# Turning the first attention's latent rows with VectorE's block transposes and HBM instead of TensorE

## The chip, the cores and the metric

The kernel runs on one core of one Trainium2 chip. The metric is device time in microseconds (us). Before the change the median of three runs is 802.17 us (801.53 to 802.32).

The engines are PE (TensorE, matmuls; PEld is its weight load), DVE (VectorE), ACT (ScalarE), POOL (GpSimd) and SP (SyncE, whose queue here issues nearly all DMAs). Each engine works through its own queue in order and waits on semaphores that other engines and DMAs set.

## The reference, cut to what matters

Two layers over 256 tokens of width 1024, all in float32. Each layer has a mixer with three branches and an MLP:

```python
for l in range(2):
    h = rms_norm(x, attn_norm[l])
    x = x + hybrid_mixer(h, ...)          # MLA | MoBA | retention, gated, then w_out
    h = rms_norm(x, mlp_norm[l])
    x = x + square(relu(h @ w_up)) @ w_down
return rms_norm(x, final_norm)

# in hybrid_mixer: p = h @ w_in, split; of it the first attention (MLA) takes 256 + 128 + 32 columns
cq, ckv = rms_norm(cq, q_norm_g), rms_norm(ckv, kv_norm_g)       # the latents, 256 and 128 wide
q = cq @ w_q_up                       # 8 heads x (64 plain + 32 for the rope)
kv = ckv @ w_kv_up                    # 8 heads x (64 key + 64 value)
k = concat(kv's key part, rope(k_rope) broadcast to all heads)
o = softmax(causal(q k^T * 96**-0.5)) v
```

`rms_norm(x, g) = x * rsqrt(mean(x^2) + eps) * g`, so a norm's weight `g` can be applied to the rows or, since it belongs to an input column of the next matmul, to the rows of the next weight matrix.

## The kernel before

**Arithmetic.** Every float32 operand of a matmul is split into a high part (rounded to the fast float32 format) and a low part (the rest), and a product is three matmuls, high by high, high by low, low by high (`three`, lines 298 to 300). A weight block arrives by DMA in `raw` (7 buffers of 128x1024), ACT copies its high part `whi` (line 277), DVE subtracts for `wlo` (line 279), both with 6 buffers; this is `fetch`. `load_w` fetches one block ahead. The order of the blocks in HBM is `weight_plan`.

**Order of the work.** A layer is a list `prog` of units. Most units are a quarter of a projection with 512 output columns: two slices of 128 rows of weights, two token tiles, three matmuls each, so 12 matmuls of 512 columns. `slot(name, j)` finds a unit and `at` hangs a step behind it. Program order gives the priorities; a planner at build time puts each engine's instructions in the order in which, by its own cost estimates, their inputs are ready, the earlier in program order first. A few places are pinned (PE's `manual_schedule`, `keep_in_program_order`, `issue_after`). So a unit's place in PE's queue is fixed when the kernel is built, and on the chip PE waits if its operands come later than planned.

**Around the change.** The units run: b0 (the 416 columns of the latents and the rope key; in the first layer within "start", together with mq), mq, mk, then mv with three units of the first attention among its quarters, then the gates gmla0, gmla1, gmoba0, gmoba1, and the rest (retention, its gate, the branches, wout, the MLP). The steps that the change touches:

- `c_copies`, `c_squares`, `c_norms`: the latent rows (token rows on partitions) in `c0`, their norms (POOL's power), the roped key copied into `krx`, and the rows scaled by their norm (DVE, line 824).
- `c_turn`: for the matmuls that follow, the latents must stand with their columns on partitions. PE transposes six 128x128 tiles of `c0` and two of `krx` into two PSUM tiles `pct` (lines 927 and 930); ACT and DVE split them to `cTh`, `cTl`, applying the norms' weights (`split` with `gain`, lines 314 and 315); ACT copies the roped key to all heads in `KK` (lines 934, 935).
- `qrope`, `qnope`, `kvup` are the units that read `cTh` and `cTl`: the query's rope part (PSUM tile `pqr`), its plain part and the keys (`nope`), the values (`pv`). `qrope` stands ahead of mv's first quarter, the others each a quarter later. `qr_rope` ropes the queries.
- `moba_rope`, `written_rows`, `read_turned`, `fetch_turned`: the second attention's queries and keys already go another way. DVE transposes rows within blocks of 32x32 (line 328), SP writes the blocks to HBM (`rowsbounce`, line 492), and four reads (line 500) bring them back so that the blocks stand in their places. `order_queries` (ACT, line 508) then puts them in order.
- `first = slot("mv", 3)`: where the first attention's first four scores stand; its other steps are counted from there.
- The end of the last layer (lines 1548 to 1568): for each of two token tiles the squares of the two halves (ACT), their multiplication by the final norm's weights (DVE), root, reciprocal, scaling (DVE 640 columns, ACT 384), and two stores.

Of the kernel before, what the change touches and what calls it, by code (L numbers as in the profile page):

```python
# [7 lines left out]
F32 = mybir.dt.float32  # L8
# [3 lines left out]
ALU = mybir.AluOpType  # L12
# [14 lines left out]
LEAD = 10  # L27

SEVEN = [(0, 1, 2, 3, 4, 6)] * L
EPS = 1e-6  # L30
GN_EPS = 1e-5
NEG_INF = -1e30
# [38 lines left out]
def weight_plan():  # L71
# [3 lines left out]
    def block(key, name, kt, cols, per):  # L75
        for j in range(0, kt, per):
            plan.append(((*key, j // per), name, (j, per), cols))
# [4 lines left out]
    for l in range(L):  # L82
# [12 lines left out]
        for i, (key, name, kt, cols) in enumerate(  # L95
            (("qrope", "mla_w_q_up", 2, C_QROPE), ("qnope", "mla_w_q_up", 2, C_QNOPE), ("kvup", "mla_w_kv_up", 1, C_KV))
        ):
            block((l, key), name, kt, cols, kt)
            plan.append(mv[i])
        plan.append(mv[3])  # L100
        for i in range(2):
            block((l, "gmla%d" % i), "w_in", KD, span(C_GMLA + 512 * i, 512), 2)
# [47 lines left out]
def trunk(ctx: ExitStack, tc: tile.TileContext, gx, wts, consts, gfin, gn, xtok, out):  # L150
# [112 lines left out]
    def fetch(key):  # L263
        if key[1] == "down" and key[2] // 4 in SEVEN[key[0]] and key[2] % 4 > 1:
            return fetch_sums(key)
        offset, n, c = where[key]
        sz = n * c
        raw = started.pop(key, None)
        if raw is None:
            raw = wp.tile([P, 1024], F32, name="raw", bufs=RAW)  # L270
            transfer(key, raw)
        hi = wp.tile([P, 1024], F32R, name="whi", bufs=6)
        lo = wp.tile([P, 1024], F32R, name="wlo", bufs=6)
        edge = {"b0mq": 416, "mq": 256}.get(key[1], sz) if key[0] == 0 else sz
        parts = (slice(0, edge), slice(edge, sz)) if edge < sz else (slice(0, sz),)
        for cs in parts:
            fetched.append(nc.scalar.activation(hi[:, cs], raw[:, cs], AF.Copy))  # L277
        for cs in parts:
            nc.vector.tensor_sub(lo[:, cs], raw[:, cs], hi[:, cs].bitcast(F32))  # L279
        return (  # L280
            hi[:, :sz].rearrange("p (k c) -> p k c", k=n),
            lo[:, :sz].rearrange("p (k c) -> p k c", k=n),
        )
# [18 lines left out]
    def gain(c):  # L302
        return G[:, c : c + 1]
# [481 lines left out]
    def layer(l, xn, before):  # L785
# [21 lines left out]
        def c_norms():  # L807
# [4 lines left out]
            for t, (ct, m) in enumerate(c0):  # L812
# [9 lines left out]
                    nc.vector.tensor_copy(dst[:, :, 16 * i : 16 * i + 16], kr[:, 0, :, :])  # L822
                for i, cs in enumerate((slice(0, MLA_QR), slice(MLA_QR, MLA_QR + MLA_KVR))):
                    nc.vector.tensor_scalar(ct[:, cs], ct[:, cs], m[:, 4 + i : 5 + i], s, op0=ALU.mult, op1=ALU.mult)

        if l:
            project(l, "b0", xn, 416, b0.extend, before, ((0,), (1,)))
# [87 lines left out]

        def c_turn():
            c["h"], c["l"] = t4("cTh"), t4("cTl")
            mla["Q"] = sb.tile([P, MLA_H, S], F32, name="Q", bufs=1)  # L920
            KK = mla["K"] = sb.tile([P, MLA_H, S], F32, name="KK", bufs=1)
            mla["v"] = [w2k("vml") for _ in range(NT)]
            pts = [misc_tile("pct") for _ in range(2)]
            for k in range(3):
                pt = pts[k // 2][:, (k % 2) * S : (k % 2) * S + S]
                for t in range(NT):
                    nc.tensor.transpose(pt[:, P * t : P * t + P], c0[t][0][:, P * k : P * k + P], ident)
            pkr = pts[1][:, S : 2 * S]
            for t in range(NT):
                nc.tensor.transpose(pkr[:, P * t : P * t + P], krx[t], ident)  # L930
            for k in range(3):
                pt = pts[k // 2][:, (k % 2) * S : (k % 2) * S + S]
                split(pt, c["h"][:, k, :], c["l"][:, k, :], gain(G_CQ + 3 * l + k))
            nc.scalar.copy(KK[0:64, 1::2, :], pkr[0:64, None, :].to_broadcast([64, 4, S]))
            nc.scalar.copy(KK[64:P, 0::2, :], pkr[64:P, None, :].to_broadcast([64, 4, S]))

        at(slot("mk", 1 if l else 2), c_turn)

        def nope(dst, w, ks, copy, bank):
            for b in range(2):  # L940
# [46 lines left out]

        project(l, "mv", xn, 512, moba_done("mv"))
        for i, unit in enumerate((qrope, qnope, kvup)):
            prog.insert(slot("mv", i), ((unit.__name__, 0), unit))  # L990
        at(slot("mv", 0), qr_rope)

        omlaT, omobaT, oretT = [], [], []
        th_mla = gates(l, "gmla", xn)
        for i, key in enumerate(("mq", "mk")):
            at(slot("mv", i), lambda key=key: moba_rope(key))
            at(slot("gmla0", 2 * i), lambda key=key: fetch_turned(key))
        first = slot("mv", 3)
        at(first, lambda: omlaT.extend((t4("omlah"), t4("omlal"))))

        def mla_scores(h0):
# [27 lines left out]
            qkT["q", h0] = in_order(qkT["mq"], h0 // 2)  # L1029

        for i in range(2):
            at(slot("gmla1", 1 + i), lambda i=i: order_queries(4 * i))
        first = slot("gmoba1", 1)
        at(first, lambda: omobaT.extend((t4("omobah"), t4("omobal"))))

# [511 lines left out]
        for t in range(NT):  # L1547
# [3 lines left out]
            for half in range(2):  # L1551
# [5 lines left out]
                square(acc, 3 * t + half)  # L1557
                if half == 0:
                    nc.vector.tensor_scalar(s2, s0, EPS, None, op0=ALU.add)
                nc.vector.tensor_mul(y[:, cs], acc, gf[:, cs])  # L1560
            nc.scalar.activation(s1, s1, AF.Sqrt, bias=s2)
            nc.vector.reciprocal(r, s1)
            cs = slice(0, 640)
            nc.vector.tensor_scalar(y[:, cs], y[:, cs], r, None, op0=ALU.mult)
            nc.sync.dma_start(out[:, t, cs], y[:, cs])
            cs = slice(640, D)
            nc.scalar.activation(y[:, cs], y[:, cs], AF.Copy, scale=r)
            nc.scalar.dma_start(out[:, t, cs], y[:, cs])
        order_pe.close()
# [116 lines left out]
```

## Time and profile before

| | |
|---|---|
| runs | 802.17 us median of 3, 801.53 to 802.32 |
| the profiled execution's own time | 802.15 us |
| its span (first to last instruction) | 800.0 us |
| mean granted TensorE clock | 0.999 of full speed |
| DVE busy | 655.9 us (82%) |
| ACT busy | 493.7 us (62%) |
| POOL busy | 29.0 us (4%) |
| DMA moved | 194.74 MB, mean 243 GB/s |

A profile is one execution. A row of a timeline reads: start in us from the span's start, duration in us, engine, line, operation, tiles written and read, sizes, count; in brackets how long the engine had been idle and what released it. Several instructions that follow each other can be merged in one row with a count. Matmuls are pipelined: one starts while the one before is in flight, so the distance between starts is what a matmul takes of PE's time, not its duration.

### The profile page before, as it was taken

Reading aid. Unit: us, or ns where it says so; the run is one execution under the profiler, and the core shown is the slowest. Engines: PE = TensorE matmul, PEld = TensorE weight load, DVE = VectorE, ACT = ScalarE, POOL = GpSimd, SP = SyncE. Lnnn points to the kernel's source line nnn. Section 1 sums busy time; section 2 is a strip of 40 time slices with the busy share of each in tenths; the row PEclk is TensorE's granted clock in tenths of the full one; section 3 lists DMA queues with packets and bytes.
Section 4 is the critical chain, followed back from the end, with each engine's and each line's share of the span. In section 5 each row is a group of like instructions: output and inputs, shape, how many; then the busy total and the mean of one; then the engine's idle time right before and its main releaser. Section 6 shows DMA issues by size and latency. Waiting matters only on the chain.

```text
span 800.0 us, 11134 instructions
## 1 busy us (share of the span) xinstructions
PE 793.3 (99%) x3818; PEld 660.3 (83%) x3818; DVE 655.9 (82%) x1131; ACT 493.7 (62%) x750; POOL 29.0 (4%) x32
## 2 busy tenths in 40 slices
PE   9999999999999999999999999999999999999997
PEld 7888887888888888888898888888888888888885
DVE  6779678878888888887796976788698879899795
ACT  7786665454557666666487865654545666666562
POOL 0100000000030000000020000000000300000000
PEclk9999999999999999999999999999999999999999
DMA  9979958965677767787746989598665687788751
GB/s 337 367 234 306 312 206 222 313 217 171 227 220 235 265 235 239 259 270 231 245 148 213 282 292 293 175 274 263 216 221 195 197 273 268 226 274 311 263 189 53
DMA packets 70280, 194.74 MB, mean 243 GB/s; under 512 B 8016, under 2 KB 28112, under 8 KB 70224
## 3 DMA queue, kind: packets, MB, share of 16 engines
q1 hardware_dynamic: 69648, 193.30, 73.2%
q10 hardware_dynamic: 576, 0.74, 0.2%
q8 instruction: 30, 0.49, 0.2%
q14 instruction: 26, 0.21, 0.1%
HBM read 171.46 MB, written 22.02 MB: 242 GB/s over the span
## 4 chain that ended last, share of the span: by engine, by line
PE 99%; ACT 0%; DVE 0%; issue 0%
PE acc L298 19%; PE acc L300 19%; PE acc L299 19%; PE pup L300 8%; PE pup L299 8%; PE pup L298 8%; PE acc L1240 6%; PE acc L859 2%; PE ps_s L1005 1%; PE po L645 1%; PE ps_s L551 1%; PE warm L765 0%; PE po L647 0%; PE b L865 0%; PE ps_r L551 0%; PE b L866 0%
## 5 line engine op out<-in xcount | busy, mean ns | idle before, releaser
L277 ACT ACTIVATE whi<-raw 128x1024 fp32r<-128x1024 f32 (+3 forms) x263 | 265.2, 1020 | 169.6 <-PE acc L300 105.9
L279 DVE TENSOR_TENSOR wlo<-raw,whi 128x1024 fp32r<-128x1024 f32 (+3 forms) x263 | 305.2, 1176 | 72.2 <-ACT whi L277 70.0
L298 PE MATMUL acc<-whi,xs 128*128 128x512 f32 (+1 forms) x384 | 150.0, 392 | 0.0
L299 PE MATMUL acc<-wlo,xs 128*128 128x512 f32 (+1 forms) x384 | 149.4, 389 | 0.0
L300 PE MATMUL acc<-whi,xs 128*128 128x512 f32 (+1 forms) x384 | 149.0, 389 | 0.0
L299 PE MATMUL pup<-wlo,xs 128*128 128x512 f32 x256 | 99.8, 390 | 0.0
L300 PE MATMUL pup<-whi,xs 128*128 128x512 f32 x256 | 99.6, 389 | 0.0
L298 PE MATMUL pup<-whi,xs 128*128 128x512 f32 x256 | 99.4, 389 | 0.0
L298 PEld LDWEIGHTS acc<-whi,xs 128*128 128x128 f32 x384 | 72.1, 188 | 15.7 <-ACT whi L277 0.7
L300 PEld LDWEIGHTS acc<-whi,xs 128*128 128x128 f32 x384 | 72.1, 188 | 14.3
L299 PEld LDWEIGHTS acc<-wlo,xs 128*128 128x128 f32 x384 | 72.1, 188 | 14.0
L300 PE MATMUL acc<-whi,sq 128*128 128x512 f32 x184 | 71.9, 391 | 0.0
L298 PE MATMUL acc<-whi,sq 128*128 128x512 f32 x184 | 71.8, 390 | 0.0
L299 PE MATMUL acc<-wlo,sq 128*128 128x512 f32 x184 | 71.6, 389 | 0.0
L300 PEld LDWEIGHTS pup<-whi,xs 128*128 128x128 f32 x256 | 48.0, 188 | 9.8
L299 PEld LDWEIGHTS pup<-wlo,xs 128*128 128x128 f32 x256 | 48.1, 188 | 9.8
L298 PEld LDWEIGHTS pup<-whi,xs 128*128 128x128 f32 x256 | 48.0, 188 | 9.8
L300 PEld LDWEIGHTS acc<-whi,sq 128*128 128x128 f32 x184 | 34.6, 188 | 7.7 <-DVE sq L319 0.6
L299 PEld LDWEIGHTS acc<-wlo,sq 128*128 128x128 f32 x184 | 34.6, 188 | 7.2
L298 PEld LDWEIGHTS acc<-whi,sq 128*128 128x128 f32 x184 | 34.5, 188 | 7.0
L573 ACT ACTIVATE prob<-prob,smx 128x128 f32<-128x128 f32 x64 | 28.3, 444 | 18.6 <-DVE smx L570 18.5
L1240 PE MATMUL acc<-mT,whi 128*128 128x512 f32 (+1 forms) x144 | 35.2, 371 | 0.0
(277 smaller groups left out, 1206.4 us busy)
## 6 DMA issues: line engine op xcount, KB each, us to landing
raw<-wts SPq DMA_DIRECT2D x264, 512.0 KB, 4.9
bounce<-hblocks SPq DMA_DIRECT2D x16, 512.0 KB, 3.8
hturned<-bounce SPq DMA_DIRECT2D x64, 128.0 KB, 3.0
pbounce<-blocks SPq DMA_DIRECT2D x8, 768.0 KB, 5.8
probT<-pbounce SPq DMA_DIRECT2D x32, 192.0 KB, 5.3
raw<-wts SPq DMA_DIRECT2D x5, 464.0 KB, 6.0
raw<-wts SPq DMA_DIRECT2D x4, 416.0 KB, 4.2
dec<-consts SPq DMA_DIRECT2D x2, 768.0 KB, 7.6
```

What stands on the lines that cost most here:

```text
L277: fetched.append(nc.scalar.activation(hi[:, cs], raw[:, cs], AF.Copy))
L279: nc.vector.tensor_sub(lo[:, cs], raw[:, cs], hi[:, cs].bitcast(F32))
L298: nc.tensor.matmul(o, ah, bh, start=start, stop=False, **more)
L299: nc.tensor.matmul(o, ah, bl, start=False, stop=False, **more)
L300: nc.tensor.matmul(o, al, bh, start=False, stop=stop, **more)
L551: mm = nc.tensor.matmul(bank[:, o], a[rows, sa], b[rows, sb_], start=True, stop=True)
L573: nc.scalar.activation(p[:, a:b], p[:, a:b], AF.Exp, bias=m[:, 2 + i : 3 + i], scale=d**-0.5, accum_out=m[:, 4 + i : 5 + i])
L645: nc.tensor.matmul(dst, vh, pT[h + j][0], start=True, stop=False)
L859: nc.tensor.matmul(mq[t][:, cs], a[:, P * t : P * t + P], wq[part][:, cs], start=first, stop=stop)
L1005: nc.tensor.matmul(bank[:, o], mla["Q"][:, h, qs], mla["K"][:, h, ks], start=True, stop=True)
L1240: nc.tensor.matmul(o, a, b, start=half == 0 and i == 0, stop=4 * half + n == KD and i == len(jobs) - 1)
```

## The change

The latent rows and the rope key are turned as the second attention's rows are: after the scaling, DVE transposes them in blocks (three tiles of 128 columns of `c0` in one instruction, `krx` in another, for each token tile), SP writes the blocks to HBM, `c_fetch` reads them back with four DMAs, and `c_turn` splits 768 columns from SBUF with one ACT and one DVE instruction, without the norms' weights; ACT puts the key in order (`kr`) and copies it to the heads. The norms' weights are applied in the splits of the weight blocks `qrope`, `qnope` and `kvup` instead (per slice of 128 rows, so the first two blocks are split in two halves).

The places move: `c_fetch` and `c_turn` have their slots, `qrope`, `qnope` and `kvup` stand one quarter of mv later, with their weight blocks one place later in the plan; the second attention's ropes, reads and ordered queries move into the gates; the first attention's scores start behind gmla0's first quarter instead of mv's last.

At the end, the last tile's second half is not multiplied by the final weights ahead of the reciprocal, but in one fused instruction with the scaling; DVE scales columns 512 to 1023, ACT 0 to 511, and the stores are 512 columns each.

```diff
+LATENT = {"qrope": 0, "qnope": 0, "kvup": 2}
@@ weight_plan
+            plan.append(mv[i])
             block((l, key), name, kt, cols, kt)
-            plan.append(mv[i])
@@ fetch
+        if key[1] in LATENT:
+            parts = [slice(c * j, c * j + c) for j in range(n)]
+            for j, cs in enumerate(parts):
+                fetched.append(split(raw[:, cs], hi[:, cs], lo[:, cs], gain(G_CQ + 3 * key[0] + LATENT[key[1]] + j))[0])
+            return tuple(part[:, :sz].rearrange("p (k c) -> p k c", k=n) for part in (hi, lo))
@@ c_norms
+            blocks = blocks_tile("c")
+            for t, (ct, _) in enumerate(c0):
+                for js, row in ((slice(0, 3), ct[:, :384]), (slice(3, 4), krx[t])):
+                    nc.vector.transpose(blocks.rearrange("p (b j t e) -> p t j b e", b=4, j=4, t=2)[:, t, js], row)
+            bounces["c"] = dr.tile([P, 4 * S], F32, name="rowsbounce", bufs=4)
+            nc.sync.dma_start(bounces["c"], blocks)
@@ c_turn
+        def c_fetch():
+            c["T"] = read_turned(bounces["c"], "cT", "exch", False)
...
-            for k in range(3):
-                pt = pts[k // 2][:, (k % 2) * S : (k % 2) * S + S]
-                for t in range(NT):
-                    nc.tensor.transpose(pt[:, P * t : P * t + P], c0[t][0][:, P * k : P * k + P], ident)
-            pkr = pts[1][:, S : 2 * S]
-            for t in range(NT):
-                nc.tensor.transpose(pkr[:, P * t : P * t + P], krx[t], ident)
...
+            split_plain(c["T"][:, 0:3].rearrange("p j t a e -> p (j t) a e"), *parts)
+            kr = w2k("kr")
+            nc.scalar.copy(kr[:, :S].rearrange("p (t a e) -> p t a e", t=NT, a=4), c["T"][:, 3])
+            for rows, odd in ((slice(0, 64), 1), (slice(64, P), 0)):
+                nc.scalar.copy(KK[rows, odd::2, :], kr[rows, None, :S].to_broadcast([64, 4, S]))
-        at(slot("mk", 1 if l else 2), c_turn)
+        at(slot("mq", 3) if l else slot("mk", 2), c_fetch)
+        at(slot("mk", 0 if l else 3), c_turn)
@@ the units and the first attention
-            prog.insert(slot("mv", i), ((unit.__name__, 0), unit))
-        at(slot("mv", 0), qr_rope)
+            prog.insert(slot("mv", i + 1), ((unit.__name__, 0), unit))
+        at(slot("mv", 1), qr_rope)
-            at(slot("mv", i), lambda key=key: moba_rope(key))
-            at(slot("gmla0", 2 * i), lambda key=key: fetch_turned(key))
-        first = slot("mv", 3)
+            at(slot("gmla0", 2 + i), lambda key=key: moba_rope(key))
+            at(slot("gmla1", 1 + i), lambda key=key: fetch_turned(key))
+        first = slot("gmla0", 0)
-            at(slot("gmla1", 1 + i), lambda i=i: order_queries(4 * i))
+            at(slot("gmoba0", i), lambda i=i: order_queries(4 * i))
@@ the last scaling
-                nc.vector.tensor_mul(y[:, cs], acc, gf[:, cs])
+                if half == 0 or t == 0:
+                    nc.vector.tensor_mul(y[:, cs], acc, gf[:, cs])
-            cs = slice(0, 640)
-            nc.vector.tensor_scalar(y[:, cs], y[:, cs], r, None, op0=ALU.mult)
-            nc.sync.dma_start(out[:, t, cs], y[:, cs])
-            cs = slice(640, D)
+            if t == 0:
+                for cs in (slice(512, 768), slice(768, D)):
+                    nc.vector.tensor_scalar(y[:, cs], y[:, cs], r, None, op0=ALU.mult)
+            else:
+                nc.vector.scalar_tensor_tensor(y[:, cs], acc, r, gf[:, cs], op0=ALU.mult, op1=ALU.mult)
+            nc.sync.dma_start(out[:, t, 512:], y[:, 512:])
+            cs = slice(0, 512)
```

## Rows read from the trace of the kernel before

**Rows 1.** The page, part 1: busy us, share of the span, instructions.
```profile
PE 793.3 (99%) x3818; PEld 660.3 (83%) x3818; DVE 655.9 (82%) x1131; ACT 493.7 (62%) x750; POOL 29.0 (4%) x32
```
**Rows 2.** PE's waits, whole span: waited for, us in total, times, longest.
```profile
PE warm L765 <- PEq L1679: 0.8, 1, 0.8
```
**Rows 3.** PE's timeline, first layer, mk's first matmul and around the transposes.
```profile
25.33 0.39 PE L298 MATMUL acc<-whi,xs 128*128 128x512 f32 x1
...
35.55 0.40 PE L298 MATMUL acc<-whi,xs 128*128 128x512 f32 x1
...
37.86 0.60 PE L927 MATMUL pct<-K,c 128*128 128x128 f32 x4
38.30 0.38 PE L930 MATMUL pct<-K,krx 128*128 128x128 f32 x2
...
38.75 0.39 PE L299 MATMUL acc<-wlo,xs 128*128 128x512 f32 x1
```
**Rows 4.** PE's timeline, second layer, around the transposes.
```profile
426.64 0.40 PE L300 MATMUL acc<-whi,xs 128*128 128x512 f32 x1
...
427.55 0.60 PE L927 MATMUL pct<-K,c 128*128 128x128 f32 x4
...
430.29 0.40 PE L300 MATMUL acc<-whi,xs 128*128 128x512 f32 x1
```
**Rows 5.** The tile pct: count, ns min/median/max, first and last start.
```profile
L927 PE MATMUL pct<-K,c x12: 270/272/273, 35.8 to 427.9; 128*128 128x128 f32 x12
```
**Rows 6.** All engines' timeline at the end of the kernel.
```profile
793.67 0.39 PE L300 MATMUL acc<-whi,sq 128*128 128x512 f32 x1
...
794.82 0.69 DVE L1560 TENSOR_TENSOR y<-acc,gf 128x512 f32<-128x512 f32 x1 [0.92 <-ACT fsq L1545]
794.82 0.29 ACT L1561 ACTIVATE fst<-fst 128x1 f32<-128x1 f32 x1
795.43 0.15 DVE L1562 RECIPROCAL fr<-fst 128x1 f32<-128x1 f32 x1
795.62 0.61 ACT L1567 ACTIVATE y<-y,fr 128x384 f32<-128x384 f32 x1 [0.50 <-DVE fr L1562]
...
796.26 0.35 ACTq L1568 DMA_DIRECT2D y<-y  x1
```
**Rows 7.** Groups by line, shapes apart, ACT: busy us, mean ns, idle before.
```profile
L888 ACT ACTIVATE mqrows<-acc,ms 128x512 f32<-128x512 f32 x4 | 2.6, 687 | 1.9 <-POOL ms L438 1.9
```
**Rows 8.** DVE's timeline: last scaled latents, first layer; last key copy, second.
```profile
37.02 0.67 DVE L824 TENSOR_SCALAR c<-c,ssc,ms 128x256 f32<-128x256 f32 x2 [0.59 <-POOL ssc L815]
...
425.90 0.26 DVE L822 COPY krx<-c 128x32 f32<-128x32 f32 x2
```
**Rows 9.** Line 328, DVE's block transposes, the second attention's queries.
```profile
L328 DVE STREAM_TRANSPOSE mqblocks<-mqrows x4: 668/685/704, 52.0 to 444.9; 128x512 f32<-128x512 f32 x4
```
**Rows 10.** SP's timeline, first layer: the queries' blocks written and read back.
```profile
53.32 0.33 SPq L492 DMA_DIRECT2D rowsbounce<-mqblocks  x1
...
58.03 1.75 SPq L500 DMA_DIRECT2D mqT<-rowsbounce  x4
```
**Rows 11.** ACT's timeline, first layer: the queries put in order.
```profile
62.67 1.14 ACT L508 COPY qkT<-mqT 128x512 f32<-128x512 f32 x2 [2.71 <-DMA mqT<-rowsbounce]
```
**Rows 12.** PE's timeline: the first matmul of pqr, first and second layer.
```profile
43.08 0.28 PE L298 MATMUL pqr<-cTh,whi 128*128 128x256 f32 x1
...
432.80 0.28 PE L298 MATMUL pqr<-cTh,whi 128*128 128x256 f32 x1
```
**Rows 13.** DVE's timeline: the first low parts of the latents, both layers.
```profile
39.87 0.87 DVE L315 SCALAR_TENSOR_TENSOR cTl<-pct,GX,cTh 128x256 fp32r<-128x256 f32 x2
...
428.62 0.48 DVE L315 SCALAR_TENSOR_TENSOR cTl<-pct,GX,cTh 128x256 fp32r<-128x256 f32 x1
```
**Rows 14.** ACT's waits, whole span: waited for, us in total, times, longest.
```profile
ACT whi L277 <- PE acc L300: 105.9, 77, 5.6
...
ACT sq L319 <- DMA hturned<-bounce: 8.3, 4, 3.2
```

More of the change, by code (lines that the diff above doesn't have):

```diff
@@ L922, in c_turn @@
             mla["v"] = [w2k("vml") for _ in range(NT)]
-            pts = [misc_tile("pct") for _ in range(2)]
-            for k in range(3):
-                pt = pts[k // 2][:, (k % 2) * S : (k % 2) * S + S]
-                for t in range(NT):
-                    nc.tensor.transpose(pt[:, P * t : P * t + P], c0[t][0][:, P * k : P * k + P], ident)
-            pkr = pts[1][:, S : 2 * S]
-            for t in range(NT):
-                nc.tensor.transpose(pkr[:, P * t : P * t + P], krx[t], ident)
[L931 to L935, printed above, removed]
-        at(slot("mk", 1 if l else 2), c_turn)
+            parts = (c[key][:, 0:3, :].rearrange("p j (t a e) -> p (j t) a e", t=NT, a=4) for key in ("h", "l"))
+            split_plain(c["T"][:, 0:3].rearrange("p j t a e -> p (j t) a e"), *parts)
[5 more added lines that the diff above has]
+        at(slot("mk", 0 if l else 3), c_turn)
         def nope(dst, w, ks, copy, bank):
```

## The prediction

> **What bounds the kernel now.** I read the page's first part, then PE's waits, then PE's timeline around the work that is removed. PE is busy 793.3 of 800.0 us, DVE 655.9, ACT 493.7 [rows 1]. Busy time alone proves little, since matmuls overlap; PE's waits do: one wait, 0.8 us, at the very start [rows 2]. So PE's queue never runs dry and the span is PE's instruction stream plus a short head and a tail of some 6 us after its last matmul. Two things follow. An instruction taken out of PE's stream is worth its pace, wherever it stood; and a wait that PE gets anywhere is paid in full, because there is no slack on PE to win it back. Work on DVE, ACT or the queues costs nothing until PE waits for it.
>
> **PE's part: sixteen transposes go.** Each layer loses eight 128x128 transposes (six of the latent rows, two of the rope key). Their price is what they add between the projection matmuls. The pace without them: from 25.33 to 35.55 us there are 45 matmuls of 512 columns, 0.227 us each [rows 3]. From 35.55 to 38.75 ten such matmuls start, with the eight transposes among them: 3.20 us for 2.27, so 0.93 us for eight, 0.116 each [rows 3]. In the second layer from 426.64 to 430.29 twelve matmuls start: 3.65 us for 2.72, again 0.93 [rows 4]. Together 1.86 us. Nothing replaces them on PE.
>
> One transpose's own duration is 272 ns [rows 5], over twice its price, because the next one starts while it is in flight. By that duration the sixteen would be worth 4.4 us; the sum goes by the pace. The Trainium skill's VectorE: DVE Perf Modes, section The three transpose paths, gives TensorE 390 ns for a (bf16) 128x128 transpose, which would make 6.2 us of them; the row is shorter and the pace shorter still, so the trace differs. The Trainium skill on the same page, section Rules for kernel authors, advises TensorE for a 128x128 transpose where PSUM will do as destination and keeps VectorE's for 32x32 blocks: a rule against this change.
>
> **What takes their place, and what hides it.** Per layer:
> - DVE transposes blocks: for each of two row tiles 384 and 128 columns. A 512-column one takes 0.685 us [rows 9], so the four cost 1.4 us (by columns) to 2.7 (if each cost a whole one); I take 1.8. DVE drops three splits from PSUM, of which two took 0.87 us [rows 13], and gets one of 768 columns instead. The balance is 1 to 2 us of DVE per layer, in stretches where PE did not wait for it: nothing. ACT exchanges three splits for one and adds a small copy: nothing. If a burst of these delayed the weight splits, their cover is that ACT's splits mostly wait for PE to free a buffer (105.9 us in 77 waits, up to 5.6 us [rows 14]), so they run a buffer or two, 3 to 5 us, ahead.
> - The norms' weights move into the splits of three weight blocks. Two of the blocks are now split in two halves: two more instructions on ACT and on DVE, at most 1.5 us each engine, same cover.
> - SP issues one write and four reads more. The nearest rows: a write at 53.32, the reads from 58.03 [rows 10], the data used at 62.67 [rows 11]: 9.35 us from issue to use, of which part was SP being busy with the next write. I take 8 to 9.35. The reads stand in SP's queue behind the write's landing, and the weight loads behind the reads; the same 7 raw buffers have to cover up to 4.7 us, a bit under two units of PE's work (a unit is 12 matmuls, 2.72 us). I cost it at nothing.
> - The head ropes, their bounces, the ordered queries and the first attention's steps are moved one to four units later. Their instructions are the same, they leave DVE free where the latents now need it, and PE has gate projections to do meanwhile. Nothing; if a queue is blocked there, the price is of the size of the waits in [rows 11, 14].
>
> **The wait that is added.** The query rope projection (pqr) now needs latents that went through HBM. First layer: the last latent scaling ends at 37.7 [rows 8], the transposes at 38.5 to 39.1, the data are back at 46.5 to 48.4, ACT's and DVE's splits (about 1 us each) end at 48.5 to 50.4. PE's queue before had pqr at 43.08 [rows 12]; less 0.93, and with the order unchanged, PE would wait 6 to 8 us. But pqr is moved behind one mv unit, and the order on PE is a planner's: it puts in front what it believes ready. Its stock is three more mv units, then the gates: mk's four units, begun at 25.33 [rows 3], end at 36.2, mv's four at 47.1, one gate unit at 49.8. Second layer: the last copy of the rope key ends at 426.2 [rows 8], data back by 435 to 437, splits by 437 to 439; PE is through mv's first unit at 434.6 (432.80 [rows 12] less 0.93 plus 2.72), through the second at 437.3, the third at 440. So the wait is 0 to 8 us in the first layer, 0 to 4.3 in the second, by where the planner puts pqr.
>
> Which? Two rows speak. Before, the planner was late: the first low part of the latents began at 39.87 and 428.62 on DVE and took under 0.5 us [rows 13], pqr ran at 43.08 and 432.80 [rows 12], 2.7 and 3.7 us behind its data. And with bounces it is early: ACT stood 2.71 us for the reads of the queries [rows 11], and four times for the MLP's, at most 3.2 us [rows 14]. A bounce late by 1 to 3 us against a margin of 2.7 and 3.7 leaves 0 to 0.5 us of wait in the first layer and none in the second. I take 0, as the middle of that lateness is under both margins.
>
> **The tail.** After the last matmul (starts 793.67) come the squares, the root at 794.82 to 795.11, and then the reciprocal, which on DVE stands behind a multiply of 0.69 us (794.82) and starts at 795.43; the scalings run 795.62 to 796.23 and the last store is issued at 796.26 [rows 6]. The multiply goes into the scaling: reciprocal at 795.15, scalings from 795.34. DVE's fused one on 512 columns of PSUM has the multiply's shape, 0.69; ACT's grows from 384 to 512 columns, 0.687 by a scaling of that size [rows 7]. Both end at 796.03, the last store goes at 796.07: 0.19 us gained. The bytes stored are the same, in two equal halves. Bounds 0 (if the fused one is slower than both) to 0.5 (if the shorter larger store counts).
>
> **Sum.** 802.15 us of the profiled execution, less 1.86, less 0.19: 800.10. The median of the runs, 802.17, is 0.02 above the profiled one, so 800.1 for the median as well. Of the 802.15 the span has 800.0; the 2.15 around it stay.
>
> **Rivals.**
> 1. *The bounce is late for pqr* (the other side). For it: 9.35 us against PE's stock of mv units, and the engine that waits is the one without slack. Against: the planner's margin, and the stock. With pqr behind three mv units in the first layer (44.4) and one in the second (434.6), PE waits some 5 and 3.5: 800.1 + 8.5 = 808.6; behind all four and one, 2.5 and 3.5, 806.1. It decides from 3.7 us in all, where the time passes 803.8. By this mechanism the Trainium skill's advice above, to leave 128x128 transposes on TensorE, would come out right; the trace of before bears it out no further than ACT's waits.
> 2. *A short wait in one layer*: 0.8 to 3.7 us, say pqr behind two mv units in the second layer (1.6) and a little in the first: 800.1 + 2 = 802.1, the gain eaten. For it: ACT's waits of 1 to 3 us on bounces [rows 11, 14]. Against: the margins.
> 3. *The change saves more than the pace*: where transposes sat alone among projections, matmuls of the new order may also run tighter, up to 272 ns for each transpose [rows 5]: 802.15 - 4.4 - 0.2 = 797.6. Against: both layers give 0.93.
>
> **Chances.** Forecast 0.55 (799.5 to 800.9); first rival 0.16; second 0.26; third 0.03. About 0.2%, 1.6 us, is what a measurement tells from no change here. Faster by more than that (under 800.57): 0.50, the forecast without its upper end plus the third; within: the second and that end, 0.33; slower: the first and the rim of the second, 0.17. The range, 799.5 to 803.8, leaves out most of the first and third, 2 in 10; the likeliest case's own is 799.5 to 800.9.
>
> **What would show it.** No pct matmul; PE's waits still 0.8 us at the start alone; no step between PE's starts over 0.45 us near pqr. The write of the latents should issue near 39 and 427, their use follow 8 to 10 us later with several mv units ahead of pqr. In the tail the reciprocal begins before 795.3 on the old scale, less 1.86. I am wrong if PE shows a wait at pqr or the nope matmuls on ACT or DVE's latent split, or if ACT, held by the read of the latents, starves PE of weight splits in the gates.

## The result, and the profile after

The changed kernel is slower: 807.43 us median of 6 runs (806.53 to 808.17) against 802.11 for the kernel before on the same chip, ratio 1.0070 with a 95% interval of 1.0059 to 1.0080. The profiled execution took 806.53 us, 804.1 of it span, against 802.15 and 800.0 before. The forecast was 800.1 and its range ended at 803.8: the sign is wrong too. The first rival, a bounce that is late for pqr, came true, but in the first layer alone. That its prices, 806.1 and 808.6, lie on both sides of the measured time is luck: they were made of 6.0 and 8.5 us of wait in two layers, and what happened is 4.0 us of wait in one and a loss behind it that no rival had.

PE's line of the page, as in [rows 1]. Sixteen matmuls fewer, and no more busy time won by it:

```profile
PE 793.6 (99%) x3802; PEld 660.4 (82%) x3802; DVE 657.8 (82%) x1139; ACT 494.0 (61%) x752; POOL 29.0 (4%) x32
```

PE's waits, against the single one of [rows 2]:

```profile
PE pqr L304 <- ACT cTh L325: 3.8, 1, 3.8
PE warm L771 <- PEq L1692: 0.8, 1, 0.8
```

The stretches around that wait (columns: stretch; length, then busy us and count of PE, PEld, DVE, ACT, POOL; granted clock; DMA share; GB/s):

```profile
36.00:46.40 10.40, 10.40 (x48) 8.54 (x46) 7.90 (x9) 4.96 (x6) 0.00 (x0) 1.00 0.94 284
46.40:50.40 4.00, 0.32 (x2) 0.00 (x0) 0.00 (x0) 0.75 (x2) 0.00 (x0) 0.85 1.07 263
50.40:56.00 5.60, 5.46 (x23) 5.26 (x24) 2.18 (x2) 4.52 (x7) 0.00 (x0) 0.50 0.35 138
56.00:64.00 8.00, 8.00 (x50) 7.20 (x49) 5.87 (x10) 7.40 (x14) 0.00 (x0) 1.00 0.74 226
```

Here is the whole loss. PE does nothing useful for 4 us, and then works for 5.6 us at a granted clock of 0.50, that is at 1.2 GHz in place of 2.4: it counts as busy, but half of it, 2.8 us at most, is lost too. The busy share of the page hides this; the clock column shows it, and so does the pace of the same matmuls of pqr, here and in a kernel of this document that keeps the full clock (the one with the reads first, below):

```profile
52.85 0.41 PE L306 MATMUL pqr<-cTh,wlo 128*128 128x256 f32 x1
53.06 0.41 PE L304 MATMUL pqr<-cTh,whi 128*128 128x256 f32 x1
```

```profile
47.41 0.28 PE L306 MATMUL pqr<-cTh,wlo 128*128 128x256 f32 x1
47.53 0.28 PE L304 MATMUL pqr<-cTh,whi 128*128 128x256 f32 x1
```

Over nine starts of 256 columns (52.85 to 54.77, and 47.41 to 48.48) a matmul takes 0.213 us here and 0.119 at the full clock. The 23 matmuls that start from 50.54 to 56.05 (21 of 256 columns, 2 of 512) take 5.51 us; at 0.119 and 0.23 they would take 2.96, so 2.55 are lost. The sum: mv's last matmul starts at 46.33 and pqr's first at 50.54, 4.21 us apart where 0.23 is the pace, so 3.98 of idle time; 806.53 - 3.98 - 2.55 = 800.00, which is the forecast but for 0.1.

The way of the latents in that stretch, from the timelines of DVE, SP, ACT and PE (start, duration, instruction, in brackets the idle time before it and what ended it), in place of [rows 12, 13]:

```profile
26.11 11.77 SPq L211 DMA_DIRECT2D raw<-wts  x7
...
37.44 0.57 DVE L834 STREAM_TRANSPOSE cblocks<-c 128x384 f32<-128x384 f32 x1
38.04 0.33 SPq L836 DMA_DIRECT2D rowsbounce<-cblocks  x1
39.15 1.52 SPq L211 DMA_DIRECT2D raw<-wts  x2
43.08 1.75 SPq L506 DMA_DIRECT2D cT<-rowsbounce  x4
...
46.33 0.39 PE L306 MATMUL acc<-whi,xs 128*128 128x512 f32 x1
49.65 0.84 ACT L325 ACTIVATE cTh<-cT 128x768 fp32r<-128x768 f32 x1 [4.55 <-DMA cT<-rowsbounce]
50.52 0.96 DVE L325 TENSOR_TENSOR cTl<-cT,cTh 128x768 fp32r<-128x768 f32 x1 [4.17 <-ACT cTh L325]
50.54 0.58 PE L304 MATMUL pqr<-cTh,whi 128*128 128x256 f32 x1 [3.83 <-ACT cTh L325]
```

Two weight loads of 512 KB each stand between the write and the reads, and the last two of the seven in the first row were issued shortly ahead of the write, at 35.18 and 37.55. From the write's issue to the first use are 11.6 us, 6.6 of them from the reads' issue. In the second layer the same steps take 8.7 and 4.6 us, and pqr, with all of mv ahead of it, does not wait:

```profile
433.52 0.33 SPq L836 DMA_DIRECT2D rowsbounce<-cblocks  x1
437.64 1.75 SPq L506 DMA_DIRECT2D cT<-rowsbounce  x4
442.21 0.85 ACT L325 ACTIVATE cTh<-cT 128x768 fp32r<-128x768 f32 x1 [3.66 <-DMA cT<-rowsbounce]
444.32 0.28 PE L304 MATMUL pqr<-cTh,whi 128*128 128x256 f32 x1
```

The end of the kernel, against [rows 6]. From the last matmul's start to the last store's issue it now takes 2.42 us, 2.59 before:

```profile
797.92 0.39 PE L306 MATMUL acc<-whi,sq 128*128 128x512 f32 x1
799.07 0.29 ACT L1571 ACTIVATE fst<-fst 128x1 f32<-128x1 f32 x1
799.39 0.16 DVE L1572 RECIPROCAL fr<-fst 128x1 f32<-128x1 f32 x1 [1.14 <-ACT fst L1571]
799.59 0.72 ACT L1580 ACTIVATE y<-y,fr 128x512 f32<-128x512 f32 x1 [0.23 <-DVE fr L1572]
799.59 0.75 DVE L1577 SCALAR_TENSOR_TENSOR y<-acc,fr,gf 128x512 f32<-128x512 f32 x1
800.34 0.38 ACTq L1581 DMA_DIRECT2D y<-y  x1
```

### The profile page after: what moved, and what is told of

The parts are those of the page before. It is cut to its first block, busy times and chain, and to the rows that moved or that the text cites. A ratio compares the mean times of both kernels' runs of the same rounds, so it can differ in the third digit from the quotient of the medians.

```text
span 804.1 us, 11122 instructions
## 1 busy us (share of the span) xinstructions
PE 793.6 (99%) x3802; PEld 660.4 (82%) x3802; DVE 657.8 (82%) x1139; ACT 494.0 (61%) x752; POOL 29.0 (4%) x32
## 4 chain that ended last, share of the span: by engine, by line
PE 92%; DMA 5%; ACT 1%; DVE 1%; SPq 0%; issue 0%; ACTq 0%
PE acc L304 18%; PE acc L306 18%; PE acc L305 18%; PE pup L306 8%; PE pup L305 8%; PE pup L304 8%; PE acc L1249 6%; DMA raw<-wts 2%; PE ps_s L1014 1%; PE po L651 1%; DMA xrow<-xtok 1%; PE ps_s L557 1%; DMA cT<-rowsbounce 1%; DMA rowsbounce<-cblocks 1%; PE po L653 0%; PE nope L304 0%
## 5 line engine op out<-in xcount | busy, mean ns | idle before, releaser
L283 ACT ACTIVATE whi<-raw 128x1024 fp32r<-128x1024 f32 (+4 forms) x257 | 259.7, 1022 | 166.2 <-PE acc L306 107.0
L285 DVE TENSOR_TENSOR wlo<-raw,whi 128x1024 fp32r<-128x1024 f32 (+4 forms) x257 | 299.2, 1179 | 65.0 <-ACT whi L283 62.0
```

## The experiments

Times are medians, each with its ratio to the kernel before on the same chip (801.9 to 802.1 throughout).

### Where the loss is: the second layer alone, and the places alone

The first kernel keeps the first layer's transposes, plan and places of before, and has the change in the second layer and in the tail.

```
-        if key[1] in LATENT:
+        if key[1] in LATENT and key[0]:
...      (the plan, c_turn, the units' places and first: as before where l == 0)
```

> The first layer is put back to the old way in everything (transposes on PE, places, plan of the weights); the second layer and the tail keep the change. Theory A (the whole loss is the first layer's wait of PE at pqr for the latents' bounce, with the lower clock that follows it): PE waits only at the start, clock 0.999, and the time is 802.1 - 0.93 - 0.15 = 801.0 us (800.6 to 801.5). Rival B (the moved steps, ropes in the gates and scores a unit later, cost something of their own in each layer): half of the 5.3 us stays, about 804.8.

Measured: 801.51 us, ratio 0.9993 (0.9984 to 1.0002), profiled 801.11. PE has one wait, at the start:

```profile
PE warm L774 <- PEq L1713: 0.8, 1, 0.8
```

The profiled execution is 1.04 us under before's, where one layer's transposes and the tail were priced at 0.93 + 0.19; the medians give 0.5, which the interval does not tell from nothing. All of the loss is in the first layer.

The second kernel has PE's transposes back in both layers, but every place, the plan and the tail as changed.

```
-        if key[1] in LATENT:
+        if False:
...      (c_turn as before, no blocks, no bounce, no c_fetch)
-        at(slot("mq", 3) if l else slot("mk", 2), c_fetch)
-        at(slot("mk", 0 if l else 3), c_turn)
+        at(slot("mk", 1 if l else 2), c_turn)
```

> The eight transposes of each layer go back to PE, with the norms' weights in the latents' splits; all the moved places, the plan of the weights and the tail stay as in the change. Theory A: no bounce, so no wait at pqr; 802.1 - 0.15 (tail) = 802.0 (801.5 to 802.5), clock 0.999. Rival B: the places cost by themselves, 804 or more, with a wait of PE or of the attention's softmax that is new against the kernel before.

Measured: 802.03, ratio 0.9999 (0.9990 to 1.0008), no wait of PE but the first. The moved ropes, scores and ordered queries cost nothing that these runs can tell, as the prediction had it; the loss belongs to the bounce.

### The price of the lower clock

Twenty matmuls of 512 columns whose result is never used are put behind mv in the first layer, all of mv ahead of pqr. At the pace of 0.227 us they take 4.5 us, about what PE waited.

```
...      (the plan and the units: all of mv ahead of qrope, qnope and kvup where l == 0)
+                if fill:
+                    filled = misc_tile("filler")
+                    for _ in range(fill):
+                        nc.tensor.matmul(filled, ah[:, :P], wh[:, per - 1, :], start=True, stop=True)
```

> The change, with twenty idle matmuls of 512 columns (0.227 us each, 4.5 us in all, results unused) in PE's queue between mv's last matmul and pqr in the first layer; qrope, qnope and kvup follow all of mv. They take the place of the wait. If the lower clock after the wait has a price of its own (in the changed kernel the granted clock is 0.50 from 50.4 to 56.0): PE stays busy, clock 1.00 throughout, and the time is 800.1 + 4.5 = 804.6, less than the changed kernel's 807.4 although PE does 4.5 us of useless work. If the clock has no price: 807.4 or more.

Measured: 806.37, ratio 1.0053 (1.0038 to 1.0069), in 4 runs. The stretches of the wait and of the half clock:

```profile
46.40:50.40 4.00, 4.00 (x19) 3.31 (x18) 0.51 (x1) 0.00 (x0) 0.00 (x0) 1.00 1.14 186
50.40:56.00 5.60, 4.50 (x30) 3.73 (x29) 0.96 (x1) 4.45 (x7) 0.00 (x0) 1.00 0.62 231
```

PE does 4.5 us of useless work, waits another 0.6 and 0.5 (the latents are later still here, first used at 51.51), and the clock stays at 1.00. By the medians this kernel is 1 us faster than the changed one, less than was expected and hardly shown: the two intervals overlap (1.0059 to 1.0080 for the changed kernel), and the profiled executions are only 0.18 us apart. What shows the price of the clock is the pace in the rows above; what this run adds is that no low clock comes where PE is kept at work in the gap. So the wait and the slow stretch behind it are two losses. The Trainium skill says the same in TensorE: Matmul & The Clock Gate, section HAM oscillation — how this bites in real kernels: a wait for a transfer amid matmuls can bring the clock back down, so that the work after it starts slow; the 0.50 above agrees.

### Why the latents are late

Four kernels change only what else the queues carry in the first layer. All of mv stands ahead of pqr in PE's queue as in the changed kernel; behind pv the planner moves the scores by a few matmuls (32 to 36 projection matmuls stand between).

First, the loads from the third block of the first gate on are put behind the write, those of the second gate behind the reads' issue.

```
-            nc.sync.dma_start(bounces["c"], blocks)
+            wrote = nc.sync.dma_start(bounces["c"], blocks)
+            if l == 0:
+                behind.setdefault((0, "gmla0", 2), []).append(wrote)
...
+            if l == 0:
+                behind.setdefault((0, "gmla1", 0), []).append(dma)
```

> The change, with the first layer's weight loads from gmla0's third block on issued behind the bounce's write, and those from gmla1's first block on behind its reads. Theory C (the bounce is slow because it shares the DMA engines with weight loads queued just ahead of it): the write lands in 3.5 to 4 us instead of 5.0, the last read 3 us after its issue instead of 5.1, PE's wait at pqr falls from 3.8 to 0.5 to 1.5 us, time 801 to 803. Rival D (the two steps take their 5 us each whatever else the engines carry): wait 3.8 us, 807.

Measured: 804.38, ratio 1.0032 (1.0023 to 1.0041). The write landed 3.0 us after its issue in place of 5.0, the reads went out at 41.19 in place of 43.08, but the data were first used only at 48.52, 7.3 us after that in place of 6.6. PE waited 2.6 us, and the expected wait of 0.5 to 1.5 did not come. The write became faster, the reads did not.

Second, the write goes out on ACT's queue, so that it is not behind anything on SP's.

```
-            nc.sync.dma_start(bounces["c"], blocks)
+            (nc.sync if l else nc.scalar).dma_start(bounces["c"], blocks)
```

> The change, with the first layer's bounce written from ACT's DMA queue instead of SP's; the reads stay on SP. Theory C in its stricter form (what delays the write are the loads ahead of it in SP's own queue): the write lands in 3 to 4 us, PE's wait falls by 1 to 2 us to 2 to 3 us, time 804.5 to 806. If the engines' whole load counts and not the queue: write 5 us as before, 807.4.

Measured: 806.38, ratio 1.0058 (1.0045 to 1.0070); the write took 6.8 us, longer than on SP's queue (SP issued three loads around it, from 37.62 to 42.47), the reads went out at 44.94, and PE waited 3.8 us as before. Another queue is no way around the loads. This agrees with the Trainium skill, DMA: Bandwidth & Descriptors, section Issuing engines are not separate DMA queues: transfers of all issuing engines run on the same sixteen DMA engines and share them.

Third, the loads of the second gate are held until the reads have landed (a small transfer out of what was read marks it); the two ahead of them, from the first gate's third block on, stay behind the write as in the first kernel.

```
+                landed = dr.tile([P, 8], F32, name="landed", bufs=1)
+                dma = nc.sync.dma_start(landed, turned[:, 0:8])
+                behind.setdefault((0, "gmla1", 0), []).append(dma)
```

> The change, with the first layer's loads held as in the run before (from gmla0's third block behind the bounce's write), and those from gmla1's first block on held until the four reads have landed (a tiny DMA on SP that reads what they wrote stands ahead of them). Theory C says that the reads are slow because weight loads share the engines with them: alone, or nearly, the last one lands 3 us after its issue, the latents' split on ACT starts at 45.5 to 46.5 instead of 49.65, PE's wait at pqr is 0 to 1 us, and the time is 800.1 to 801.5. Theory D (reads of this shape take 5 us after all): the split starts near 48.5, as with the loads held behind the reads' issue, wait 2.6 us, 804.4.

Measured: 804.84, ratio 1.0037 (1.0024 to 1.0050), PE waited 2.2 us: a miss for theory C and near the numbers of D. Nothing was queued behind the reads, and they still took 6.2 us from 42.37 to their first use at 48.62. At that point the reads looked slow by themselves. (With loads behind them as well, in the first kernel, it was 7.3, so what is queued behind also counts for something.) But two loads were still ahead of them, and the rows from 40 to 46 us show 291 to 315 GB/s: 1 MB ahead of the reads takes some 3.4 us at that rate.

```profile
39.77 1.22 SPq L211 DMA_DIRECT2D raw<-wts  x2
42.37 1.76 SPq L936 DMA_DIRECT2D cT<-rowsbounce  x4
```

Fourth, those two are held as well: the same mark, two blocks earlier, in place of the hold behind the write.

```
-                behind.setdefault((0, "gmla1", 0), []).append(dma)
+                behind.setdefault((0, "gmla0", 2), []).append(dma)
```

> The changed kernel, with the two weight loads that stand on SP's queue between the latents' write and its reads in the first layer (issued 39.15 to 40.67) held until the reads have landed; PE's order is the changed kernel's. Theory F: the reads need 6.6 us from first issue to use (43.08 to 49.65), against 4.6 in the second layer (437.64 to 442.21), because these 1 MB go ahead of them: moved at the 300 or so GB/s of the rows from 40 to 46 they take 3.3 us, and the reads get their turn late. Then the use of cT comes at 47.2 to 47.7, PE's wait at pqr shrinks from 3.8 to 1.4 to 2.0 us, and the time is 804.0 to 805.2 (less of a clock loss as well). Rival G: reads of 32 partitions are slow here whatever is queued: use near 49.5, wait 3.8, 807. Rival H: held weights are missed later: a new wait of PE behind a split in the gates, time 806 or more though pqr comes early.

Measured: 802.88, ratio 1.0018 (1.0009 to 1.0027). The changed kernel's 5.3 us over the kernel before have become 1.0, and that is better than expected. But four loads are issued later, and not the two of the expectation: the two that went out at 35.18 and 37.55, ahead of the write, wait here as well as the two between write and reads. Five loads and not seven go out from 26 us to the write, none from there to the reads:

```profile
38.18 0.33 SPq L836 DMA_DIRECT2D rowsbounce<-cblocks  x1
40.81 1.75 SPq L934 DMA_DIRECT2D cT<-rowsbounce  x4
45.71 6.38 SPq L211 DMA_DIRECT2D raw<-wts  x7
```

Against the third kernel, which differs in the two loads between write and reads alone, the data are used 4.5 us after the reads' issue in place of 6.2. The transfers of the stretch from 36 to 62 us (issues, KB of each, median us from issue to landing), first the changed kernel, then this one:

```profile
rowsbounce<-cblocks SPq DMA_DIRECT2D x1, 512.0 KB, 5.0
cT<-rowsbounce SPq DMA_DIRECT2D x4, 128.0 KB, 4.6
qkoth<-qr SPq DMA_DIRECT2D x4, 64.0 KB, 2.3
```

```profile
rowsbounce<-cblocks SPq DMA_DIRECT2D x1, 512.0 KB, 2.6
cT<-rowsbounce SPq DMA_DIRECT2D x4, 128.0 KB, 3.0
qkoth<-qr SPq DMA_DIRECT2D x4, 64.0 KB, 7.4
```

The write takes 2.6 us in place of 5.0, each read 3.0 in place of 4.6, the latents are first used at 45.29, 4.4 us earlier, and the wait at pqr is all but gone. Part of the loss comes back later: the swap of qr's halves now stands behind the seven loads that go out once the reads have landed and takes 7.4 us in place of 2.3, and PE waits for Q:

```profile
PE ps_s L1022 <- DVE Q L1002: 1.6, 1, 1.6
...
PE pqr L305 <- DVE cTl L325: 0.2, 1, 0.2
```

### More stock on PE instead

The other way is to give PE more to do while the latents are away. Four kernels put all of mv and one or two quarters of the first gate ahead of pqr in the first layer.

```
+        if l == 0:
+            plan += mv + gmla[:AHEAD_GATES]
...
+            prog.insert(slot("mv", i + 1) if l else slot("gmla0", AHEAD_GATES), ((unit.__name__, 0), unit))
...
-        first = slot("gmla0", 0)
+        first = slot("gmla0", 0 if l else 2)
```

Two quarters, loads as changed:

> The change, with the first layer's program order and weight plan altered: all of mv and two quarters of gmla0 stand ahead of qrope, qnope and kvup, the scores behind gmla0's third quarter. The bounce is left as slow as it is. Theory A (the loss is PE's in-order wait at pqr and nothing else): pqr stands 5.4 us later in PE's queue, the data are there first, PE waits at the start alone, clock 0.999, and the time is 802.1 - 1.86 - 0.15 = 800.1 (799.7 to 800.7). Rival E (the later first attention then waits elsewhere: its softmax or its values, which PE reads at a fixed place): a new wait of PE of 1 to 4 us behind 80 us, 801 to 805.

Measured: 805.51, ratio 1.0046 (1.0033 to 1.0059). The wait at pqr shrinks to 0.2, 0.3 us come at pv, and 3.0 us stand at the scores instead:

```profile
PE ps_s L1019 <- DVE Q L1000: 3.0, 1, 3.0
```

Two quarters, the loads held as in the first kernel of the section before, and the scores one unit later (first is gmla0's unit 3):

> Two quarters of the first gate ahead of pqr in the first layer, its scores one unit later still than in the run with gates first (ahead of the second gate's first quarter instead of the first gate's last), and the loads held as in the run with held loads. What was left there was one wait of 3.0 us at the scores for Q. One unit is 2.72 us: the theory that waits are moved and not removed until the whole chain behind the latents has its lateness covered gives a wait of 0.3 us or none, full clock, 800.1 to 801.2. Rival: ACT's queue (copies of the rope key, mv's copies, weight splits) grows with each unit put ahead and the scores wait again, 2 to 3 us, 803 to 805.

Measured: 805.74, ratio 1.0057 (1.0043 to 1.0071), a miss: 3.2 us at the scores still. qr was copied on ACT only at 57.94, behind the splits of weights, the swap went out at 59.14, behind eight loads that SP issued over 15.4 us, and took 6.5 us. (The profile puts this wait down to a weight split on ACT, which ended at the same time as the first of Q's parts on DVE.) The scores were later, and so was all that leads to them.

One quarter, loads held in that way:

> Both remedies, each in part: one quarter of gmla0 ahead of qrope, qnope and kvup in the first layer (scores behind gmla0's second quarter), and the loads held behind the bounce's write and reads. Data at 49.3 as with the loads held alone, pqr at 49.1: wait 0 to 0.5 us, clock 0.999, time 800.1 to 800.8. If the held loads make the weights late in the gates, PE waits there for a weight split on ACT or DVE: 801 to 803.

Measured: 804.11, ratio 1.0029 (1.0018 to 1.0040), above both expectations: 0.6 us at pqr, and 1.5 at nope, whose bank of PSUM was to be emptied by mv's copies, which stood on ACT behind the wait for cT:

```profile
PE nope L310 <- ACT mv L854: 1.5, 1, 1.5
```

One quarter, with the reads first:

> The two loads held as in the run beside it, and in the first layer all of mv and one quarter of the first gate put ahead of pqr, as in the run with one gate quarter ahead. By theory F the latents' parts are ready at 48.3 to 48.8, PE's stock ends at 49.1, and mv's copies on ACT come ahead of nope's need (they stood behind the wait for cT, 1.5 us, in the run with one gate quarter and the loads only partly held): no wait of PE but the 0.8 at the start, full clock from 36 to 80 us, time 800.1 to 801.0. Rival G (reads slow by themselves): as with one gate quarter ahead, 804.1. Rival H (weights missed later): one new wait of 1 to 3 us in the gates, 802 to 804.

Measured: 802.52, ratio 1.0006 (0.9997 to 1.0015), a miss. In the profiled execution, at 804.58 the slowest of the eleven, there is no wait at pqr, 0.2 at nope and 1.9 at the scores, behind the swap. Stock helps only to where the next late transfer is due.

### The last wait

What was open now was whether the wait at the scores has the same cause as the one at pqr. Time for it first: the reads-first kernel with first one unit later in the first layer.

```
-        first = slot("gmla0", 0)
+        first = slot("gmla0", 0 if l else 1)
```

> The run with the reads first, its only left wait (1.6 us at the scores for Q, whose other halves of qr came back on SP's queue 9 us after they were copied) given one unit of 12 matmuls more: the first layer's scores one unit later. Theory F (the time lost is the lateness of small transfers behind queued weight loads, and nothing else) expects no wait but the start's 0.8, and the time of the reads-first run less 1.6 to 1.9: 800.9 to 801.3, that is the second layer's half of the gain and nearly all of the first's. Rival (a wait is only moved on): another wait of 1 to 3 us behind the scores, 802.5 or more.

Measured: 804.16, ratio 1.0024 (1.0011 to 1.0036), in 7 runs. The edit did not do what it was for: the planner left the first scores where they were, 34 projection matmuls behind pv, and the wait is 2.0 us. But it gives a pair. The stretch behind the wait, in this kernel and in the reads-first kernel:

```profile
64.00:68.00 4.00, 4.00 (x16) 3.39 (x15) 3.91 (x7) 0.00 (x0) 0.00 (x0) 0.57 0.00 0
```

```profile
64.00:68.00 4.00, 4.00 (x22) 3.13 (x21) 3.91 (x6) 0.34 (x1) 0.00 (x0) 1.00 0.00 0
```

Waits of 2.0 and 1.6 us at one place, and in these two executions one is followed by a low clock and the other is not. Then the cause: the loads of the second gate go behind the swap's issue, so that two loads stand ahead of it in place of seven.

```
             mla["qo"] = swapped(mla["qr"])
+            if l == 0:
+                behind.setdefault((0, "gmla1", 0), []).append(swapping[-1])
```

> The reads-first run, with the weight loads from the second gate on held behind the issue of qr's swap in the first layer too (2 loads of 512 KB ahead of the swap in place of 6 or 7); the scores where they were. Theory F expects the swap back some 4 to 6 us after its issue near 51.5 instead of 9, Q ready near 60, no wait at the scores, 800.6 to 801.3. Rival (the swap is slow for another reason, as it moves from partitions to partitions on one chip): landing still near 60, wait of 1 to 1.6 us or more, 802.5 to 803. Rival H: the held loads leave a unit of the gates without weights, a wait of 1 to 3 us there.

Measured: 800.64 (800.34 to 801.45, 11 runs), ratio 0.9985 (0.9976 to 0.9994), profiled 800.62: faster than the kernel before. Transfers from 36 to 62 us, and PE's waits:

```profile
cT<-rowsbounce SPq DMA_DIRECT2D x4, 128.0 KB, 3.0
qkoth<-qr SPq DMA_DIRECT2D x4, 64.0 KB, 2.0
```

```profile
PE warm L774 <- PEq L1705: 0.8, 1, 0.8
PE pqr L305 <- DVE cTl L325: 0.2, 1, 0.2
```

The swap takes 2.0 us, the scores don't wait, though they stand four matmuls earlier than in the reads-first kernel (30 behind pv), the clock is 1.00 from 40 to 76 us. Last, the same with one quarter of the first gate ahead of pqr and the scores one unit later.

> As the run beside it, with one quarter of the first gate ahead of pqr in the first layer (2.72 us more stock on PE while the latents are under way). No wait at pqr, at nope 0 to 0.3, at the scores none if the swap is back by 62: 800.4 to 801.2. If it isn't faster than the run beside it, the 0.2 us of wait at pqr there were all that stock could win.

Measured: 800.63, ratio 0.9984 (0.9975 to 0.9992): no faster. The stock is not needed when the transfers are on time. Between the changed kernel and the one that also holds the loads for the swap lie 6.7 us (5.3 above and 1.4 below the kernel before), and no arithmetic: only when SP issues the loads of the first 60 us, and what the planner makes of it.

## Why the prediction was wrong

- *PE's part, 1.86 us, and the tail, 0.19*: right. The tail gave 0.17. The transposes' worth shows in the second layer alone (1.04 in the profile with the tail) and in the best kernel: 1.53 of the 2.05 forecast in the profiled execution, 1.38 by the medians. What is missing lies at pqr, and is more than the 0.2 that the list of waits shows: the 48 matmuls of pqr and nope take 6.37 us there (46.33 to 52.70, where pv starts), and at 0.119 each they would take 5.71, so 0.66 are lost. Why the kernel with more stock, which loses 0.23 there (49.72 to 55.66), is no faster stays open.
- *The moved steps, the norms' weights and DVE's blocks at nothing*: right for the places, by the run with the transposes back.
- *The second layer's wait, none*: right, but by the planner, which put all four units of mv ahead (pqr at 444.32), not by the margin that I argued with; the write went out at 433.52, where I had it near 427 (DVE copied the last of the rope key at 432.38, in place of 425.90 [rows 8]), and the data were used at 442.21.
- *The first layer: "I take 0, as the middle of that lateness is under both margins"*: the step that failed. The planner did put all of mv ahead of pqr, so the margin was already in the order, and it then put nothing more. The right ends stood in the working: splits at 50.4 and mv's end at 47.1 make 3.3 us, against the 3.8 measured. But I set them aside for a lateness of 1 to 3 us, taken from ACT's waits for other bounces, whose consumers stand elsewhere in the order and which say nothing of this one's margin. That 50.4 came so near the measured 50.5 is luck: the blocks were ready half a microsecond to 1 us earlier than I had them (38.0), pqr began after ACT's split alone, and the way through HBM was 2.3 us longer than the longest that I took.
- *The term that was mis-sized*: "I take 8 to 9.35" for write to use, out of one row of another bounce [rows 10, 11]. It was 11.6 in the first layer, and 8.7 in the second. I named what stands in SP's queue behind the reads (weight loads, costed at nothing) and not what stands ahead: two loads of 512 KB shortly before the write and two between write and reads. With these four held the latents are first used 4.4 us earlier (49.65 to 45.29), and the time over the kernel before falls from 5.3 us to 1.0.
- *The clock*: no term at all. I priced a wait "in full", at its own length; 3.98 us of it drew 2.55 more behind it.
- The sentence that PE has no slack to win a wait back was right, and should have weighed more: with all of mv in front both ends of the working (splits at 48.5 and 50.4, mv's end at 47.1) gave a wait, and 0.16 for the first rival was too little. The Trainium skill's rule from VectorE: DVE Perf Modes, section Rules for kernel authors, to leave 128x128 transposes on TensorE, came out right for the kernel as changed (807.43 against 802.11). It is not a rule about the transposes themselves: with the loads in another order the changed kernel gains 1.4 us, some 0.2 of it by the tail.

## What to carry to other kernels

Where work leaves a saturated engine for a way through memory, read the queue ahead of each transfer, not only behind it: in these runs a small transfer that someone waited for took some of the time of the large ones issued just before it, and the fix was to issue those later. Compare when its data are due with the end of the work that is certain to stand in front, and believe that difference rather than the habits of other bounces. And price a wait of the matrix engine of some microseconds at more than its length: nine of the ten kernels here with one of 1.5 to 3.8 us had a lower clock behind it.

## What the runs showed of the hardware

- A read of 128 KB took 4.6 us behind two loads of 512 KB (4.8 in the third kernel, with nothing queued behind the reads) and 3.0 without; a swap of 64 KB 7.4 us behind seven loads and 2.0 behind two that had landed.
- The write of 512 KB took 5.0 us with loads issued 2.9 and 0.5 us ahead of it (35.18, 37.55) and two behind, 3.0 with two behind alone, 2.6 with none, and 6.8 on ACT's queue.
- Ten of the kernels here have a wait of PE of 1.5 to 3.8 us. In the 4 us behind it the mean granted clock was 0.50 to 0.64 in nine of them, but 1.00 behind 1.6 us, where 2.0 at the same place gave 0.57. It was 1.00 too where the 4 us were filled with idle work. Most of the ten also scatter more from run to run (802.44 to 806.25 with 2.0 us at the scores, 800.34 to 801.45 without a wait there), but not all (805.31 to 805.82 with 3.0).
